# Layer 1's first modulation chunks and the context's keys and values, computed in the experts' stage instead of the tail

## The chip, the cores and the metric

One NeuronCore of a Trainium2 chip runs the whole program. The metric is device time in microseconds of one execution, as the median of several; times inside an execution are read from a profile of one execution, in microseconds from its first instruction.

## The reference, cut to what matters

Two blocks of a model follow each other, on 256 tokens of width 1024, all in fp32. The first block ends in a mixture of 16 experts; its result x is normalised and enters the second block, which has two layers and a second stream of 256 tokens, the context. The context does not depend on x. Layer 0 uses an MLA attention, layer 1 a neighbourhood attention (NA):

```python
for i in range(DEPTH_2):                      # 2 layers
    need_ctx = i < DEPTH_2 - 1                # only in layer 0
    mod   = (silu(c) @ ada_w[i] + ada_b[i])[:, None, :]
    mod_c = silu(c_ctx) @ ada_w[i] + ada_b[i]
    sh1, sc1, g1, sh2, sc2, g2 = split(mod, 6)       # and csh1, csc1, ... from mod_c
    h  = x * (1 + sc1) + sh1
    hc = ctx * (1 + csc1) + csh1
    y, yc = mixer(h, hc, ...)                 # layer 1: keys and values from h and from hc
    x = layer_norm(alpha * x + g1 * y)
    if need_ctx: ctx = layer_norm(alpha * ctx + cg1 * yc)
    x = layer_norm(alpha * x + g2 * mlp(x * (1 + sc2) + sh2))
    if need_ctx: ctx = layer_norm(alpha * ctx + cg2 * mlp(ctx * (1 + csc2) + csh2))

# NA mixer: qkv = t @ w_qkv + b_qkv for t = h and for t = hc; of hc only keys and values are used here
```

`ada_w[i]` is 1024 x 6144; the kernel cuts its columns into 12 chunks of 512. Chunks 0 to 3 are shift and scale of the attention (sh1, sc1), 4 and 5 its gate, 6 to 11 the same for the MLP. `w_qkv` is 1024 x 3072; the kernel cuts it into 4 pieces of 256 columns each for queries (part 0), keys (part 1) and values (part 2), 1024 KB a piece.

## The kernel before, in words

The program has three stages, and each engine works through its instructions in the order in which the program issues them.

- **Front** (`front`): first attention, router, layer 0's modulation.
- **Experts** (`experts`, line 1002): for each of 16 experts, gate and up weights in 8 pairs of 1408 KB tiles, then 11 tiles of 1024 KB of the down weights. All are loaded on SyncE's (SP's) queue through six buffers. Matmuls of 32 gathered rows (`egg`, `egu`, `ey`) use each tile once. Between them runs a generator, `ctx_stream` (line 1713): layer 0 for the context, that is MLA, output projection, norm, and the MLP. Its weights are loaded through `weight_loads` (line 304), four buffers `cwt` of 1024 KB, on GpSimd's queue. The generator is pulled in step with the experts: `context(units)` lets it take `CTX_STEPS` steps, spread evenly from expert 0's fifth pair to the start of the last expert. The matmuls of this stream are full-precision fp32. At its end the context is stored to DRAM as `ctx2`.
- **Tail** (`tail`, line 1906): what depends on x: layer 0's MLA and MLP, layer 1's NA and MLP. Here operands are split: a weight tile `cwt` is cast by ScalarE to a high part `wh` (L387), VectorE subtracts to get the low part `wl` (L388), activations have the same two parts, and `mm` (lines 176 to 178) issues three fp32r matmuls in place of one. Two or three places hold converted weights at a time (`slot`, `set_slots`, `weight`).

In the tail a second generator, `filler` (line 1767), is pulled between other work: four times in MLA (`MLA_PULLS`), once in its output projection (`PROJ_PULLS`), once in the hand-over to the MLP, then once for each step of the MLP. It computes layer 1's modulation (`ada`, line 426) with two buffers `adaw`: six chunks (`ADA_VECTOR`) on TensorE, one chunk a pull (8 matmuls `adap`, and 4 small ones `adac` that collect the chunk before), then six on VectorE, eight steps each. At its end it loads `ctx2` and makes the modulated context `hcT` (transposes `mtr`, ScalarE, GpSimd).

A hand-over between two parts of the tail is a `Between`: as output pieces of one part finish, VectorE adds the residual and takes the statistics; ScalarE normalises token half 0 (`xacc`, L1244); `finish` then transposes it (`mtx`), ScalarE and GpSimd make high and low parts (`hTx`), and the same follows for token half 1, with VectorE helping. `before()` and `between()` in `finish` are the places for other TensorE work. In the hand-over from the first MLP to NA they hold the context's value groups 0 and 1: `before` all of group 0, `between` all of group 1. After it come the values of x for these two weights, and then for each of the other two value weights and four key weights one group for the context and one for x (`na_proj`, tile `nqkv`), 48 matmuls of 256 columns each. Then come the queries and the attention itself.

Of the kernel before, what the change touches and what calls it, by code (L numbers as in the profile page):

```python
# [106 lines left out]
PROJ_PULLS = (0, 0, 1, 0, 0, 0, 0)  # L107
ADA_VECTOR = 6
# [5 lines left out]
CTX_STEPS = 109  # L114
# [42 lines left out]
def drain(gen):  # L157
    for _ in gen:
        pass


class Kernel:
# [141 lines left out]
    def weight_loads(self):  # L304
# [39 lines left out]
        mlp("c", 0, nc.gpsimd)  # L344
        lw.hold = len(lw.items)
# [79 lines left out]

    def ada(self, layer, pool, nbuf, loader, q, q2, vector=12):
# [4 lines left out]
        for ch in range(12):  # L431
# [12 lines left out]
        o, _ = COLS["adab"]  # L444
        bcol = self.cols[:, o + 48 * layer:o + 48 * layer + 48]

        def collect(ch, m, rhs):

            kind, half = divmod(ch, 2)
            nw = rhs.shape[1]  # L450
            p = self.bank(self.ada_tag, [128, 4, 2], "adac")
            for i in range(4):
                nc.tensor.matmul(p[:, i, :nw], m[:, i * 128:i * 128 + 128], rhs, start=True, stop=True)
            for i in range(nw):
                nc.vector.scalar_tensor_tensor(mod[:, ch * 4:ch * 4 + 4, i], p[:, :, i],
                                               1.0 if kind in (1, 4) else 0.0, bcol[:, ch * 4:ch * 4 + 4],
                                               op0=OP.add, op1=OP.add)
            if ch in (5, 11):
                gates.append(ch)
# [17 lines left out]
        for ch in range(vector):  # L477
# [1235 lines left out]
    def ctx_stream(self):  # L1713
# [48 lines left out]
        self.ctx2 = self.dram.tile([128, 2, D], F32, name="ctx2")  # L1762
        nc.gpsimd.dma_start(self.ctx2, x)
        yield


    def filler(self):
# [7 lines left out]
        c2 = None  # L1775
        for ch in ag:
            if ch == 4:
                self.modulation("c1a", 1, (0, 1), 1, "l2g0", "l2b0")
                self.modulation("x1a", 1, (0, 1), 0, "l2g0", "l2b0")
            if ch == ADA_VECTOR and c2 is None:  # L1780
                c2 = self.s8([128, 2, D], "c2")
                nc.scalar.dma_start(c2, self.ctx2)
            yield
        self.modulation("x1m", 1, (3, 4), 0, "l1g1", "l1b1")
        self.hcT = [self.fp.tile([128, 8, 256], F32R, name="hcT" + n, tag="adaw", bufs=2) for n in "hl"]
        t = self.cm["c1a"]
        for k in range(0, 8, 2):
            p = self.transpose_to(c2, k, 2, "c", "mtr")
            for j in (k, k + 1):
# [423 lines left out]
```

## Time and profile before

| | us |
|---|---|
| median of three runs | 2369.21 (2366.24 to 2371.48) |
| profiled execution | 2369.5 |
| its span, first to last instruction | 2367.4 |
| TensorE matmul busy | 2009.7 (85%) |
| VectorE busy | 801.4 (34%) |
| ScalarE busy | 552.3 (23%) |
| GpSimd busy | 253.6 (11%) |
| HBM read, over the span | 783.23 MB, 332 GB/s |

PE is TensorE's matmul side, PEld its weight load, DVE VectorE, ACT ScalarE, POOL GpSimd, SP SyncE. Busy times include what overlaps, so matmuls listed at 0.28 us may start every 0.12 us; starts tell more than durations. A full-precision fp32 matmul is listed as more than one record. The granted clock is the share of TensorE's full speed. L176 is line 176 of the kernel.

### The profile page before, as it was taken

To read this page: it belongs to the slowest core of one execution; us is meant where nothing else is said; L and a number is where in the kernel's file an instruction comes from. 1 tells how busy PE (TensorE), PEld (TensorE's weight loads), DVE (VectorE), ACT (ScalarE), POOL (GpSimd) and SP (SyncE) were. 2 spreads that over 40 slices of the span, in tenths; PEclk is the share of its full clock that TensorE was granted. 3 is DMA by queue.
4 is the path that set the end of the run, shared out by engine and by line. 5 is a ranking of instruction groups with operands and counts; after the bars stand their busy time and mean duration, and the time that the engine had idled before them with its cause. 6 is when DMAs were issued, how large, how long until landed. Compare 5 with 4: busy or idle time off the path is not lost.

```text
span 2367.4 us, 31973 instructions
## 1 busy us (share of the span) xinstructions
PE 2009.7 (85%) x13612; PEld 1244.8 (53%) x13612; DVE 801.4 (34%) x1471; ACT 552.3 (23%) x993; POOL 253.6 (11%) x274
## 2 busy tenths in 40 slices
PE   7998778787768877877878778678999999998998
PEld 6864324343214333332333333225888999987997
DVE  5643111121211111111111111214557765377555
ACT  5432011121000000000000000004444453276443
POOL 2021000000010000000000000003212113233001
PEclk9998888999968888988888889769999999999999
DMA  9879999999999999999999999998538864334652
GB/s 344 325 293 372 421 416 419 421 417 422 415 410 419 417 396 420 416 413 418 417 418 418 399 419 417 422 423 327 210 134 276 276 222 130 96 106 151 205 178 90
DMA packets 170006, 787.59 MB, mean 333 GB/s; under 512 B 13280, under 2 KB 73928, under 8 KB 113288
## 3 DMA queue, kind: packets, MB, share of 16 engines
q1 hardware_dynamic: 145432, 694.96, 74.1%
q0 software_dynamic: 24288, 89.54, 10.3%
q8 instruction: 107, 1.75, 0.3%
q10 hardware_dynamic: 144, 1.05, 0.1%
q14 instruction: 35, 0.29, 0.0%
HBM read 783.23 MB, written 2.27 MB: 332 GB/s over the span
## 4 chain that ended last, share of the span: by engine, by line
PE 46%; DMA 39%; DVE 3%; ACT 2%; issue 1%; DVEq 0%; ACTq 0%
DMA wg<-in_w_up 30%; DMA wd<-in_w_down 10%; PE egu L1045 4%; PE ey L1092 4%; PE acc L176 3%; PE acc L178 3%; PE acc L177 3%; PE ph L177 3%; PE ph L176 3%; PE ph L178 3%; PE py L174 2%; PE egg L1045 2%; PE ph L174 2%; PE nqkv L176 2%; PE nqkv L177 2%; PE nqkv L178 2%
## 5 line engine op out<-in xcount | busy, mean ns | idle before, releaser
L1045 PE MATMUL egu<-wg,xeT 128*32 128x352 f32 x2048 | 220.4, 557 | 112.3 <-DMA wg<-in_w_up 112.3
L388 DVE TENSOR_TENSOR wl<-cwt,wh 128x1024 fp32r<-128x1024 f32 (+1 forms) x202 | 249.1, 1276 | 57.0 <-ACT wh L387 56.8
L1092 PE MATMUL ey<-wd,hT 128*32 128x512 f32 x1408 | 197.6, 668 | 71.0 <-DMA wd<-in_w_down 70.5
L1045 PE MATMUL egg<-wg,xeT 128*32 128x352 f32 x2048 | 200.4, 514 | 62.4 <-DMA wg<-in_w_gate 62.3
L387 ACT CAST wh<-cwt 128x1024 fp32r<-128x1024 f32 (+2 forms) x218 | 214.7, 1035 | 91.3 <-issue 49.1
L1045 PEld LDWEIGHTS egu<-wg,xeT 128*32 128x32 f32 x2048 | 65.9, 123 | 246.6 <-DMA wg<-in_w_up 167.8
L1575 ACT ACTIVATE hu<-ph 128x512 f32<-128x512 f32 x48 | 28.7, 598 | 551.8 <-PE ph L174 442.1
L1045 PEld LDWEIGHTS egg<-wg,xeT 128*32 128x32 f32 x2048 | 57.5, 116 | 188.3 <-DMA wg<-in_w_gate 94.4
L176 PE MATMUL ph<-hTxh,wh 128*128 128x256 f32 x512 | 146.8, 287 | 1.6 <-ACT hTxh L1193 1.6
L177 PE MATMUL ph<-hTxl,wh 128*128 128x256 f32 x512 | 146.6, 286 | 0.6 <-DVE hTxl L1196 0.5
L178 PE MATMUL ph<-hTxh,wl 128*128 128x256 f32 x512 | 146.2, 286 | 0.0
L1092 PEld LDWEIGHTS ey<-wd,hT 128*32 128x32 f32 x1408 | 35.5, 115 | 195.2 <-DMA wd<-in_w_down 115.3
L1596 DVE TENSOR_TENSOR accc<-accc,py 128x512 f32<-128x512 f32 x60 | 41.3, 688 | 280.8 <-PE py L174 280.8
L174 PE MATMUL ph<-hcT,cwt 128*128 128x256 f32 x512 | 135.4, 423 | 0.0
L174 PE MATMUL py<-cwt,hs 128*128 128x512 f32 x256 | 132.5, 665 | 0.0
L174 PEld LDWEIGHTS ph<-hcT,cwt 128*128 128x128 f32 x512 | 106.5, 214 | 43.7 <-issue 27.6
L1578 DVE SCALAR_TENSOR_TENSOR hs<-ph,hu 128x512 f32<-128x512 f32 x16 | 11.1, 692 | 308.9 <-ACT hu L1575 308.9
L314 POOL DMA_DIRECT2D cwt<-in_w x32 | 25.8, 806 | 803.8 <-PE ph L174 334.4
L176 PEld LDWEIGHTS ph<-hTxh,wh 128*128 128x128 f32 x512 | 99.3, 194 | 2.8 <-ACT hTxh L1193 2.3
L177 PEld LDWEIGHTS ph<-hTxl,wh 128*128 128x128 f32 x512 | 99.2, 194 | 1.7 <-issue 0.7
L178 PEld LDWEIGHTS ph<-hTxh,wl 128*128 128x128 f32 x512 | 99.3, 194 | 0.0
L176 PE MATMUL acc<-wh,hsh 128*128 128x512 f32 (+1 forms) x256 | 97.8, 382 | 0.0
(562 smaller groups left out, 3491.9 us busy)
## 6 DMA issues: line engine op xcount, KB each, us to landing
wg<-in_w_gate SPq DMA_DIRECT2D x128, 1408.0 KB, 17.8
wg<-in_w_up SPq DMA_DIRECT2D x128, 1408.0 KB, 19.0
wd<-in_w_down SPq DMA_DIRECT2D x176, 1024.0 KB, 14.3
cwt<-in_w SPq DMA_DIRECT2D x64, 1024.0 KB, 5.3
cwt<-in_w POOLq DMA_DIRECT2D x32, 1024.0 KB, 13.7
adaw<-in_ada_w SPq DMA_DIRECT2D x24, 1024.0 KB, 9.2
adaw<-in_ada_w POOLq DMA_DIRECT2D x24, 1024.0 KB, 7.9
cwt<-in_w_in SPq DMA_DIRECT2D x12, 1024.0 KB, 10.5
```

Of the source, the lines that this page charges most:

```text
L174: t.matmul(out, L[0], R[0], start=start, stop=stop, **kw)
L176: t.matmul(out, L[0], R[0], start=start, stop=False, **kw)
L177: t.matmul(out, L[0], R[1], start=False, stop=False, **kw)
L178: t.matmul(out, L[1], R[0], start=False, stop=stop, **kw)
L314: q.dma_start(v, src)
L387: (high or nc.scalar.copy)(parts[0][:, s], t[:, s])
L388: (eng or self.low_eng).tensor_tensor(parts[1][:, s], t[:, s], parts[0][:, s].bitcast(F32), op=OP.subtract)
L1045: nc.tensor.matmul(ps[n][h][32 * j:32 * j + 32, :352], xeT[:, k, e * CAP:(e + 1) * CAP], w[:, c0:c0 + 352], start=k == 0, stop=k == 7, ski ...
L1092: nc.tensor.matmul(py[h][32 * s:32 * s + 32, :], hT[:, r, q], w[:, u, h * 512:h * 512 + 512], start=n < 2, stop=n >= 9, skip_group_check=True)
L1575: nc.scalar.activation(u, p, AF.Relu)
L1578: nc.vector.scalar_tensor_tensor(h, p, 0.0, u, op0=OP.max, op1=OP.mult)
L1596: nc.vector.tensor_add(s, s, p)
```

## The change

Chunks 0 to 3 of layer 1's modulation leave the filler and become steps of the context stream, after its MLP. They are computed on TensorE as before, and the helper that collects a chunk is now shared (`ada_collect`). The filler's `ada` starts at chunk 4; chunks 4 and 5 are still done on TensorE, the rest on VectorE. The pulls stay where they are.

The context stream goes on: it modulates the context (`hcT3`, one fp32 part instead of two) and multiplies it with the four key and the four value pieces of `w_qkv`, in full-precision fp32. Keys get their bias and are split into high and low parts (`kc`), values get theirs (`vc1`), and all go to DRAM. The store of `ctx2` goes. `weight_loads` gets 16 more items for it, on GpSimd's queue. `CTX_STEPS` grows from 109 to 132.

In the tail the context's eight groups go, with the modulated context and its load. Three loads bring `vn` and `kc` from DRAM. In the hand-over to NA, `before` holds nothing, and `between` holds the first half (token half 0) of x's value groups 0 and 1; the second halves follow after the hand-over. The conversion of the weights for x stays.

```diff
--- before.py
+++ after.py
@@ -105,13 +105,14 @@
 ADA_PULLS = (0, 1, 0, 2, 0, 0, 2, 0, 0, 2, 0, 0, 1, 0, 1, 1, 1, 1)
 MLA_PULLS = (3, 9, 13, 16)
 PROJ_PULLS = (0, 0, 1, 0, 0, 0, 0)
+ADA_FIRST = 4
 ADA_VECTOR = 6
 WOUT_AT = (14, 15)
 
 UNITS = 11, 4, 8 * 11 + 11 * 4
 CTX_FROM = 5 * 11
 CTX_LEFT = 8 * 11 + 11 * 4
-CTX_STEPS = 109
+CTX_STEPS = 132
 
 
 class Loader:
@@ -342,6 +343,13 @@
             add(("f", "wout", i), (2, 1024), self.kp(a["w_out"], i * 256, 2, 0, 1024), nc.sync)
         mla("c", nc.gpsimd)
         mlp("c", 0, nc.gpsimd)
+        for ch in range(ADA_FIRST):
+            for h in range(2):
+                add(("c", "ada", ch, h), (4, 512), self.kp(a["ada_w"][1], h * 512, 4, ch * 512, 512), nc.gpsimd)
+        for part in (1, 2):
+            for i in range(4):
+                add(("c", "qkv", part, i), (8, 256),
+                    self.kp(a["na_w_qkv"], 0, 8, part * 1024 + i * 256, 256), nc.gpsimd)
         lw.hold = len(lw.items)
         mla("x", nc.sync)
         mlp("x", 0, nc.sync)
@@ -423,12 +431,27 @@
             o, w = COLS[n]
             nc.scalar.activation(self.sc32[:, :, i], self.cols[:, o:o + w], AF.Silu)
 
+    def ada_collect(self, layer, ch, m, rhs):
+
+        nc = self.nc
+        mod = (self.mod0, self.mod1)[layer]
+        o, _ = COLS["adab"]
+        bcol = self.cols[:, o + 48 * layer:o + 48 * layer + 48]
+        nw = rhs.shape[1]
+        p = self.bank(self.ada_tag, [128, 4, 2], "adac")
+        for i in range(4):
+            nc.tensor.matmul(p[:, i, :nw], m[:, i * 128:i * 128 + 128], rhs, start=True, stop=True)
+        for i in range(nw):
+            nc.vector.scalar_tensor_tensor(mod[:, ch * 4:ch * 4 + 4, i], p[:, :, i],
+                                           1.0 if ch // 2 in (1, 4) else 0.0, bcol[:, ch * 4:ch * 4 + 4],
+                                           op0=OP.add, op1=OP.add)
+
     def ada(self, layer, pool, nbuf, loader, q, q2, vector=12):
 
         nc = self.nc
         W = 6144
         w = self.a["ada_w"][layer]
-        for ch in range(12):
+        for ch in range(ADA_FIRST, 12):
             for h in range(2):
                 src = bass.AP(tensor=w.tensor, offset=w.offset + h * 512 * W + ch * 512,
                               ap=[[W, 128], [128 * W, 4], [1, 512]])
@@ -441,20 +464,9 @@
         yield
         mod = (self.mod0, self.mod1)[layer]
         sel = self.tab("sel")
-        o, _ = COLS["adab"]
-        bcol = self.cols[:, o + 48 * layer:o + 48 * layer + 48]
 
         def collect(ch, m, rhs):
-
-            kind, half = divmod(ch, 2)
-            nw = rhs.shape[1]
-            p = self.bank(self.ada_tag, [128, 4, 2], "adac")
-            for i in range(4):
-                nc.tensor.matmul(p[:, i, :nw], m[:, i * 128:i * 128 + 128], rhs, start=True, stop=True)
-            for i in range(nw):
-                nc.vector.scalar_tensor_tensor(mod[:, ch * 4:ch * 4 + 4, i], p[:, :, i],
-                                               1.0 if kind in (1, 4) else 0.0, bcol[:, ch * 4:ch * 4 + 4],
-                                               op0=OP.add, op1=OP.add)
+            self.ada_collect(layer, ch, m, rhs)
             if ch in (5, 11):
                 gates.append(ch)
 
@@ -474,7 +486,7 @@
                                      ap=[[128, 8], [2048, nw], [1, 128]]), r[:8 * nw])
 
         last = None
-        for ch in range(vector):
+        for ch in range(ADA_FIRST, vector):
             p = self.bank(self.ada_tag, [128, 512], "adap")
             gate_rows()
             for h in range(2):
@@ -1759,9 +1771,58 @@
         g2 = [self.row(self.modrow[0], (2 + 1) * 1024 + hf * 512, 512, 2) for hf in range(2)]
         yield from self.resid_norm(x, [acc[:, tt].rearrange("p (a b) -> a p b", a=2) for tt in range(2)], 0, 1, 1,
                                    lambda hf: g2[hf])
-        self.ctx2 = self.dram.tile([128, 2, D], F32, name="ctx2")
-        nc.gpsimd.dma_start(self.ctx2, x)
-        yield
+
+        sw = self.sw
+        for ch in range(ADA_FIRST):
+            p = self.bank("c", [128, 512], "adap")
+            for h in range(2):
+                t = self.lw.take(("c", "ada", ch, h))
+                for g in range(4):
+                    nc.tensor.matmul(p[32 * g:32 * g + 32, :], self.sc32[:, 4 * h + g, :], t[:, g],
+                                     start=h == 0, stop=h == 1, skip_group_check=True)
+                self.lw.done(("c", "ada", ch, h))
+            m = sw.tile([128, 512], F32, name="adam", tag="qn", bufs=2)
+            self.copy(m, p)
+            yield
+            self.ada_collect(1, ch, m, self.tab("sel"))
+        self.modulation("c1a", 1, (0, 1), 1, "l2g0", "l2b0")
+        self.modulation("x1a", 1, (0, 1), 0, "l2g0", "l2b0")
+        hT = self.fm(8, False, None, "hcT3")
+        yield from self.modulate(hT, x, "c1a", "c")
+        self.kc = [self.dram.tile([128, 8, 256], F32R, name="kc" + n) for n in "hl"]
+        self.vc1 = self.dram.tile([128, 2, D], F32, name="vc1")
+        for part in (1, 2):
+            for i in range(4):
+                if part == 2 and i % 2 == 0:
+                    b = self.row(a["na_b_qkv"], 2048 + i * 256, 512, 2)
+                w, f = self.weight(("c", "qkv", part, i), False)
+                p = self.bank("c", [128, 2, 256], "nkv")
+                for j in range(2):
+                    js = slice(j * 128, j * 128 + 128)
+                    for k in range(8):
+                        if part == 1:
+                            self.mm(p[:, j], [w[0][:, k, js]], [hT[0][:, k]], k == 0, k == 7)
+                        else:
+                            self.mm(p[:, j], [hT[0][:, k, js]], [w[0][:, k]], k == 0, k == 7)
+                    if j == 0:
+                        yield
+                f()
+                if part == 1:
+                    hi = sw.tile([128, 2, 256], F32R, name="nkh", tag="qn", bufs=2)
+                    lo = sw.tile([128, 2, 256], F32R, name="nkl", tag="mptS", bufs=2)
+                    for j in range(2):
+                        bk = self.col("bqkv", 8 + 2 * i + j)
+                        nc.scalar.activation(hi[:, j], p[:, j], AF.Identity, bias=bk)
+                        nc.vector.scalar_tensor_tensor(lo[:, j], p[:, j], bk, hi[:, j].bitcast(F32),
+                                                       op0=OP.add, op1=OP.subtract)
+                    nc.gpsimd.dma_start(self.kc[0][:, 2 * i:2 * i + 2], hi)
+                    nc.gpsimd.dma_start(self.kc[1][:, 2 * i:2 * i + 2], lo)
+                else:
+                    vs = sw.tile([128, 2, 256], F32, name="nv", tag="qn", bufs=2)
+                    c0 = i % 2 * 256
+                    nc.vector.tensor_tensor(vs, p, b[:, None, c0:c0 + 256].to_broadcast([128, 2, 256]), op=OP.add)
+                    nc.gpsimd.dma_start(self.vc1[:, :, i * 256:i * 256 + 256], vs)
+                yield
 
 
     def filler(self):
@@ -1772,26 +1833,9 @@
         next(ag)
         lf.pump()
         yield
-        c2 = None
         for ch in ag:
-            if ch == 4:
-                self.modulation("c1a", 1, (0, 1), 1, "l2g0", "l2b0")
-                self.modulation("x1a", 1, (0, 1), 0, "l2g0", "l2b0")
-            if ch == ADA_VECTOR and c2 is None:
-                c2 = self.s8([128, 2, D], "c2")
-                nc.scalar.dma_start(c2, self.ctx2)
             yield
         self.modulation("x1m", 1, (3, 4), 0, "l1g1", "l1b1")
-        self.hcT = [self.fp.tile([128, 8, 256], F32R, name="hcT" + n, tag="adaw", bufs=2) for n in "hl"]
-        t = self.cm["c1a"]
-        for k in range(0, 8, 2):
-            p = self.transpose_to(c2, k, 2, "c", "mtr")
-            for j in (k, k + 1):
-                f = self.tw.tile([128, 256], F32, name="fullc", tag="full", bufs=3)
-                nc.scalar.activation(f, p[:, j - k], AF.Identity, bias=t[:, 1, j:j + 1], scale=t[:, 0, j:j + 1])
-                nc.scalar.copy(self.hcT[0][:, j], f)
-                nc.gpsimd.tensor_sub(self.hcT[1][:, j], f, self.hcT[0][:, j].bitcast(F32))
-            yield
 
     def na_attention(self, q, kvc, kvx):
         nc = self.nc
@@ -2080,23 +2124,27 @@
                     ql.append(self.tw.tile([128, 4, 256], F32R, name="ql" + n, tag="t4" + n, bufs=1))
                 return qh[:, t], ql[t // 4][:, t % 4]
 
-            def context(part, i):
-                w, f = self.weight(("x", "qkv", part, i), True)
-                return self.na_proj(w, None, part, i, self.hcT, (kct, self.vn)[part - 1], "c"), w, f
-
-            gc, w0, f0 = context(2, 0)
-            gc1, w1, f1 = context(2, 1)
-            hT = bt.finish(0, "ln2_b", lambda: drain(gc), lambda: drain(gc1))
+            nc.sync.dma_start(self.vn, self.vc1)
+            for t, d in zip(kc, self.kc):
+                nc.gpsimd.dma_start(t, d)
+            ww = [self.weight(("x", "qkv", 2, i), True) for i in range(2)]
+            gv = []
+
+            def values():
+
+                for i, (w, f) in enumerate(ww):
+                    gv.append(self.na_proj(w, f, 2, i, bt.hT, v, "d"))
+                    next(gv[i])
+            hT = bt.finish(0, "ln2_b", between=values)
         with ExitStack() as e1:
             self.sw = self.pool(e1, "naw")
             att = self.na_attention(qt, (kct, self.vn), (kxt, v))
-            drain(self.na_proj(w0, f0, 2, 0, hT, v, "d"))
-            drain(self.na_proj(w1, f1, 2, 1, hT, v, "d"))
+            for g in gv:
+                drain(g)
             next(att)
             for part, dst in ((2, v), (1, kxt)):
                 for i in range(2 if part == 2 else 0, 4):
-                    gc, w, f = context(part, i)
-                    drain(gc)
+                    w, f = self.weight(("x", "qkv", part, i), True)
                     drain(self.na_proj(w, f, part, i, hT, dst, "d"))
                     pull(bt.rest, 2)
             nat = self.pool(e1, "nat")
```

## Rows read from the trace of the kernel before

**Rows 1.** Busy time by stage; columns: stage, length, engines, granted clock, DMA share, GB/s.

```profile
205.00:1590.00 1385.00, 1087.78 (x7011) 450.56 (x7006) 217.73 (x420) 94.36 (x202) 47.29 (x55) 0.86 1.01 416
...
1800.00:1970.00 170.00, 170.00 (x1093) 154.39 (x1092) 119.74 (x145) 79.96 (x102) 25.64 (x29) 1.00 0.75 252
...
1970.00:2066.00 96.00, 93.86 (x787) 93.42 (x786) 40.81 (x62) 29.10 (x50) 30.80 (x35) 1.00 0.34 104
...
2066.00:2150.00 84.00, 78.44 (x805) 68.32 (x804) 63.09 (x149) 64.19 (x139) 24.49 (x28) 1.00 0.31 88
```

**Rows 2.** Waits: engine and line, what it waited for, us, times, longest.

```profile
PE egu L1045 <- DMA wg<-in_w_up: 112.3, 70, 3.5
...
PE ey L1092 <- DMA wd<-in_w_down: 70.5, 56, 3.0
```

**Rows 3.** DMA queues of 546 to 606: packets, MB, share of 16 engines.

```profile
q1 hardware_dynamic: 2941, 25.18, 100.6%
```

**Rows 4.** The same for 886 to 1328.

```profile
q1 hardware_dynamic: 18997, 165.14, 90.3%
q0 software_dynamic: 4887, 18.84, 10.7%
```

**Rows 5.** The same for the whole execution.

```profile
q0 software_dynamic: 24288, 89.54, 10.3%
```

**Rows 6.** Timeline of TensorE in the experts' stage: start, length, what, records.

```profile
1444.69 3.72 PE L174 MATMUL ph<-hcT,cwt 128*128 128x256 f32 x16
...
1595.55 1.38 PE L1092 MATMUL ey<-wd,hT 128*32 128x512 f32 x8
```

**Rows 7.** Timeline of TensorE from the MLP's last matmul to the third context group.

```profile
1969.66 0.28 PE L176 MATMUL nqkv<-wh,hcTh 128*128 128x256 f32 x1
...
1975.40 1.04 PE L1178 MATMUL mtx<-tabs,xacc 128*128 128x128 f32 x8
...
1981.97 0.60 PE L1178 MATMUL mtx<-tabs,xacc 128*128 128x128 f32 x4
...
1994.86 0.28 PE L176 MATMUL nqkv<-wh,hcTh 128*128 128x256 f32 x1
```

**Rows 8.** Timeline of ScalarE and VectorE among the key projections.

```profile
2031.46 0.47 ACT L1706 ACTIVATE kxh<-nqkv,cols 128x256 fp32r<-128x256 f32 x1 [4.20 <-PE nqkv L178]
...
2033.93 2.36 DVE L388 TENSOR_TENSOR wl<-cwt,wh 128x1024 fp32r<-128x1024 f32 x2 [0.45 <-ACT wh L387]
```

**Rows 9.** Timeline of ScalarE and GpSimd in the hand-over.

```profile
1973.00 1.24 ACT L1244 ACTIVATE xacc<-xacc,bmv 128x1024 f32<-128x1024 f32 x1 [0.43 <-DVE bmv L1243]
...
1981.05 0.74 POOL L1196 TENSOR_TENSOR hTxl<-full,hTxh 128x256 fp32r<-128x256 f32 x1 [0.41 <-ACT hTxh L1193]
...
1986.33 0.73 POOL L1196 TENSOR_TENSOR hTxl<-full,hTxh 128x256 fp32r<-128x256 f32 x1 [0.56 <-DVE hTxh L1193]
```

**Rows 10.** Busy time of 4 us after two other hand-overs.

```profile
1780.00:1784.00 4.00, 3.84 (x19) 3.87 (x20) 3.84 (x5) 3.19 (x4) 0.74 (x1) 0.57 0.98 380
...
2172.00:2176.00 4.00, 2.82 (x13) 2.18 (x14) 2.38 (x8) 3.04 (x8) 2.31 (x3) 0.63 0.76 255
```

**Rows 11.** Timeline of TensorE: modulation chunks, what follows one, context transposes.

```profile
1690.68 1.92 PE L483 MATMUL adap<-adaw,sc 128*32 128x512 f32 x16
...
1693.45 1.07 PE L1473 MATMUL mpt<-tabs,meb 128*128 128x128 f32 x8
...
1759.91 1.92 PE L483 MATMUL adap<-adaw,sc 128*32 128x512 f32 x16
...
1772.89 1.99 PE L483 MATMUL adap<-adaw,sc 128*32 128x512 f32 x16 [0.20 <-ACT full L1186]
...
1937.04 0.60 PE L246 MATMUL mtr<-tabs,c 128*128 128x128 f32 x4
```

**Rows 12.** DMA issues: times, KB each, median us from issue to landing.

```profile
cwt<-in_w POOLq DMA_DIRECT2D x32, 1024.0 KB, 13.7
...
cwt<-in_na_w_qkv SPq DMA_DIRECT2D x12, 1024.0 KB, 5.3
```

## The prediction

> **What bounds the kernel now.** I read the table of stages first [rows 1]. The kernel has three parts: a front that ends near 205 us, the experts' stage until about 1600, the tail. In the experts' stage (205 to 1590) the 16 DMA engines are busy all the time (share 1.01, 416 GB/s), TensorE only 1088 of 1385 us at a mean clock of 0.86. The waits say who is waited for: TensorE stood still for weight tiles, 112 and 71 us in the two longest [rows 2]. So this stage lasts as long as its bytes take, and TensorE has about 297 us to spare in it. The tail is the reverse: 170 of 170 us of TensorE in the second MLP part, 93.9 of 96 where queries, keys and values are projected, DMA at 0.31 to 0.75 [rows 1]. There every microsecond of TensorE work is one of the kernel, if the next work is ready.
>
> So the change moves work from where TensorE is the limit to where DMA is. It must be priced twice: bytes added to a stage that has no DMA time left, against matmul time taken out of the tail.
>
> **What it adds to the experts' stage.** Sixteen loads of 1024 KB (8 of modulation weights, 8 of key and value weights), 16.78 MB; two broadcast rows of 256 KB, 0.52 MB; twelve stores of 256 KB (key high and low parts, values), 3.15 MB; one store of 1024 KB, the old context, goes: 1.05 MB less. Net 19.4 MB, all on GpSimd's queue.
>
> The price of a byte there. In 546 to 606 only SP's queue runs: 25.18 MB in 60 us, 2.38 us/MB [rows 3]. In 886 to 1328 both run: 165.14 MB of SP's cost 165.14 x 2.383 = 393.5 us, so the 18.84 MB of GpSimd's queue took the other 48.5 us, 2.57 us/MB [rows 4]. They are of the same kind as the added ones (1 KB to 4 KB rows, 1024 KB each), so I take it: 19.4 x 2.57 = **49.9 us**. From below 2.38 us/MB, 46.2 us; from above the whole-kernel share of that queue, 10.3% of 2367.4 us for 89.54 MB [rows 5], 2.72 us/MB, 52.8 us. I exclude that they cost nothing, because no slice of that stage has DMA time free.
>
> The work that comes with them: a step of eight full-precision matmuls takes TensorE 3.72 us (16 records) [rows 6]; eight weights of two steps make 59 us, four modulation chunks of 2.77 us (below) 11. That is 70 of 297 us to spare, and it costs nothing as long as the loads stay the limit; without that cover it is 70 us. On VectorE and ScalarE it is a few copies per step, beside 218 and 94 busy us of 1385 [rows 1]. The stream still ends at the last expert's start, since the step count that paces it and its steps both grow by 23. A store of keys waits for ScalarE and VectorE, and the next weight load stands behind it on GpSimd's queue; four buffers run ahead, so I put that at nothing.
>
> **What it removes from the tail.** (a) Context keys and values. One group is 48 matmuls. Durations (0.28 us) overlap, so I read starts: 1969.66 to 1975.40 is one group, **5.74 us** [rows 7]. Eight go, 45.9 us. Six of them stand in the dense run of projections: 6 x 5.74 = 34.4 us come back in full, if the conversion of the next weight still fits under the 5.74 us of the one group that is left to each weight. From the free slot (2031.46) to the last VectorE piece (2033.93 + 2.36) it takes 4.8 us [rows 8], so it just does; if VectorE is held up by another 0.9 us, the rest is paid six times.
>
> (b) The other two cover the hand-over from MLP to attention, and here the cover goes. Before: from 1969.66 to 1994.86 TensorE does two context groups, transposes and two value groups, 25.2 us, without a long stop [rows 7]. After: nothing is there at 1969.66. The normalised half is ready at 1973.00 + 1.24 = 1974.2 [rows 9]. The transposes may start there and not at 1975.40; the chain of ScalarE and GpSimd pieces, whose last lasts until 1981.79 [rows 9], ends 1.1 us earlier, 1980.7. The first half of value group 0 trails it (ends about 1981), the first half of group 1 follows (2.9), then the other transposes (1.1), near 1984 to 1985. From the start of these transposes to the last low half it took 1981.97 to 1987.06, 5.1 us [rows 7, 9]; so the second half of group 0 ends about 1989.2 and that of group 1 about 1992.1. The stretch shrinks by 2.8 us instead of 11.5. And TensorE has stood almost idle for some 11 us: after the like hand-overs the granted clock fell to 0.57 and 0.63 over 4 us (part of it at 1.2 GHz) [rows 10]. Half the clock doubles the 2.9 us of a half group; I take 2.3 of it as lost. So **0.5 us** is gained here, bounds -3 (both halves slow) and +2.8.
>
> (c) Modulation. The first four of the six chunks on TensorE go. One takes 1690.68 to 1693.45, 2.77 us [rows 11], four 11.1. But the pulls stay where they were, and the later ones now pull VectorE steps. Gone from TensorE are those at 1690.68 (in a softmax chain, where VectorE's rotation of the queries would be late next; I count 1 of 2.77), at 1759.91 (between output pieces, in full), at 1772.89 (inside the hand-over before the MLP, where TensorE waits for the normalised rows anyway; 0.5), and one among dense projections (in full): 1 + 2.77 + 0.5 + 2.77 = **7 us**, bounds 4 and 11.
>
> (d) The context's transposes, four sets near 0.5 us in the dense MLP [rows 11]: **2 us**.
>
> New in the tail are three loads of 1024 KB (keys twice, values), at a DMA share of 0.34; they are needed at the first scores, more than 60 us later. SP's and GpSimd's queues wait with them for the MLP input's buffers at most, free before the hand-over: nothing. If that cover were gone, 5.3 us each, what one load takes to land in this stretch [rows 12].
>
> Sum: 34.4 + 0.5 + 7 + 2 = 43.9 us out (38 to 50), 49.9 in (46 to 53). The profiled execution took 2369.5 us (span 2367.4), the median of three is 2369.2, the same for this purpose. 2369.5 + 49.9 - 43.9 = **2375.5 us**. What three runs can tell from no change is 0.2%, 4.7 us: faster is below 2364.5, slower above 2374.
>
> **Rivals.**
> A, the forecast: bytes are paid in full, the hand-over opens. 2371 to 2383. Chance 0.60; 0.47 of it above 2374.
>
> B, it ends faster: all removed matmul time comes back, because the hand-over closes up by itself (the values start as soon as the rows are there). 45.9 + 11.1 + 2 = 59 us out: 2360.4. It decides from 54.6 us on. For it: 6 of 8 groups lie in dense work. Against it: the 4.6 us from 1969.66 to 1974.2 in which nothing is ready. 0.13.
>
> C, no change: bytes at SP's price, the hand-over at its better bound and modulation at 9: 2369.5 + 46.2 - 48.2 = 2367.5. 0.16.
>
> D: loads pay their time to land, not their share: 16 x 5.3 = 85 us [rows 12] and about 7 for the rest, 2418. Against it: in the experts' stage loads took 13.7 us to land [rows 12] with all engines busy, so they overlap. 0.03.
> The Trainium skill has a rule that points this way ("DMA: Bandwidth & Descriptors", section "Anatomy of one DMA"): a fixed cost of some 2 us and bytes over 436 GB/s for each transfer. By it a load is an estimated 4.4 us, sixteen are 70 and not 43, and the sum would be near 2403. By that rule 27 us more than forecast would show; the trace doesn't bear it out, its 2.57 us/MB [rows 4] are 2.7 us for such a load.
>
> E: two modulation loads per step, at 13.7 us each [rows 12], are more than a step lasts (1385 us by 132 steps, 10.5); chunks 2 and 3 hold TensorE some 13 us each, and the experts behind it don't catch up: 2375.5 + 26 = 2401. Against it: TensorE is free a fifth of the stage, and six tiles wait in buffers. 0.06.
>
> F: the loads hide, the experts' stage stays as long: 2369.5 - 43.9 = 2325.6. Against it: share 1.01. 0.02.
>
> **Numbers.** Predicted 2375.5. The range 2362 to 2386 takes in A, C and half of B. Faster 0.13 + 0.02 = 0.15; same 0.13 + 0.16 = 0.29; slower 0.47 + 0.03 + 0.06 = 0.56.
>
> **What would show it.** The last expert's first down-projection near 1645 and not 1595.55 [rows 6], with DMA still at 1.0; the tail from there to the end some 44 us shorter; a TensorE idle stretch of 4 to 5 us right after the MLP, low clock behind it; 5.7 us for each weight in the key and value projections. Wrong if the experts' stage grows by clearly less than 46 us (a cheaper byte) or more than 53, if projections wait for the weight conversion (then slower still), or if values close the gap.

## The result, and the profile after

The changed kernel takes 2392.71 us in the median (2389.18 to 2395.99, four runs) against 2368.82 for the kernel before on the same chip: ratio 1.0101, interval 1.0089 to 1.0114. It is 23.9 us slower; 6 were forecast, and the range ended at 2386. The profiled execution took 2395.99 us (span 2394.2), 3.3 us over the median; what is known of these 3.3 is told below.

The stages of the changed kernel, columns as in [rows 1]:

```profile
205.00:1645.00 1440.00, 1152.31 (x7327) 499.19 (x7325) 231.84 (x456) 93.34 (x206) 68.11 (x84) 0.86 1.00 411
...
1865.00:2028.00 163.00, 163.00 (x1031) 147.14 (x1030) 113.19 (x137) 71.63 (x84) 17.71 (x20) 1.00 0.76 258
2028.00:2092.00 64.00, 54.61 (x403) 52.95 (x403) 37.70 (x51) 25.13 (x42) 33.04 (x35) 0.89 0.50 154
```

Its longest waits for weights, as in [rows 2]:

```profile
PE egu L1057 <- DMA wg<-in_w_up: 114.1, 75, 3.5
...
PE ey L1104 <- DMA wd<-in_w_down: 51.8, 37, 3.5
```

GpSimd's queue over the whole execution, as in [rows 5]:

```profile
q0 software_dynamic: 28240, 102.65, 11.6%
```

13.1 MB more on that queue: 19.4 more in the stage, 2.1 of reloaded keys more and 8.4 of modulation weights less in the tail. So the bytes were counted rightly. But the stage (to 1645) moves 411 GB/s, not 416, although it is still the one that waits for weights.

To split the 26.8 us between the spans I use one mark: the last expert's first scatter matmul, where the tail begins. Before:

```profile
L1926 PE MATMUL esc<-sgye x8: 592/592/592, 1618.4 to 1621.4; 128*128 128x512 f32 x8
```

After:

```profile
L1970 PE MATMUL esc<-sgye x8: 592/592/592, 1683.3 to 1686.3; 128*128 128x512 f32 x8
```

The stage ends **64.9 us later** (49.9 forecast; the last expert's first down-projection starts at 1659.1 where 1645 was named); from the mark to the end of the span the tail went from 749.0 to 710.9 us, **38.1 us shorter** (43.9 forecast). The larger miss is in the experts' stage, so most experiments are about that.

**Where the stage loses time.** I cut it into windows of 4 us and added up what is missing in the DMA share wherever it is under 0.93: before 2.8 us in 3 windows, after 9.9 us in 11. One such place, TensorE of the changed kernel where an expert turns from its gate/up tiles (`egg`, `egu`) to its down tiles (`ey`):

```profile
1076.53 2.58 PE L1057 MATMUL egu<-wg,xeT 128*32 128x352 f32 x16 [0.84 <-DMA wg<-in_w_up]
1079.04 5.37 PE L175 MATMUL py<-cwt,hs 128*128 128x512 f32 x8
1087.16 1.24 PE L1083 MATMUL eht<-tabs,hh 128*128 128x128 f32 x8 [2.75 <-DVE hh L1075]
...
1089.45 1.94 PE L1104 MATMUL ey<-wd,hT 128*32 128x512 f32 x8
1091.32 4.37 PE L175 MATMUL ph<-hcT,cwt 128*128 128x256 f32 x16
```

VectorE there:

```profile
1082.72 0.69 DVE L1608 TENSOR_TENSOR accc<-accc,py 128x512 f32<-128x512 f32 x1 [17.03 <-PE py L175]
1084.44 0.69 DVE L1608 TENSOR_TENSOR accc<-accc,py 128x512 f32<-128x512 f32 x1 [1.03 <-PE py L175]
1085.05 2.05 DVE L1075 TENSOR_TENSOR hh<-hh,egu 128x352 f32<-128x352 f32 x4
```

ScalarE had its factor of `hh` ready:

```profile
1075.76 0.46 ACT L1073 ACTIVATE hh<-egg 128x352 f32<-128x352 f32 x1 [0.66 <-PE egg L1057]
```

Engines and DMA in the next windows:

```profile
1086.00:1090.00 4.00, 2.42 (x15) 1.70 (x19) 2.34 (x7) 0.79 (x3) 0.00 (x0) 0.91 1.01 414
1090.00:1094.00 4.00, 4.00 (x17) 2.31 (x10) 0.23 (x1) 0.26 (x1) 0.00 (x0) 0.67 0.68 231
1094.00:1098.00 4.00, 4.00 (x32) 1.95 (x34) 0.00 (x0) 0.00 (x0) 0.00 (x0) 1.00 0.57 195
```

SyncE's waits from 1075 to 1110:

```profile
SPq L999 <- PE ey L1104: 17.7, 4, 11.9
```

Read them as a chain. The last `egu` ends at 1079.1, and both factors of `hh` are there. A step of the context (`py`) takes TensorE at 1079.04. VectorE takes its instructions in the order of issue, and the step's two sums (`accc`) were issued before `hh`; they wait for `py`, so `hh` begins at 1085.05, six us late. The first down tile is used at 1089.45, and a second step holds TensorE until 1095.6. All six weight buffers are full meanwhile, SyncE waits 11.9 us for one, and the DMA share falls to 0.57. The Trainium skill ("PSUM — Partial Sum Buffer", section "Engine vs sequencer instructions") calls VectorE's queue strictly first in, first out; these rows agree.

### The profile page after: what moved, and what is told of

The parts are those of the page before. It is cut to its first block, busy times and chain, and to the rows that moved or that the text cites. A ratio compares the mean times of both kernels' runs of the same rounds, so it can differ in the third digit from the quotient of the medians.

```text
span 2394.2 us, 31753 instructions
## 1 busy us (share of the span) xinstructions
PE 2031.6 (85%) x13484; PEld 1251.1 (52%) x13484; DVE 810.9 (34%) x1479; ACT 540.1 (23%) x973; POOL 264.9 (11%) x289
## 3 DMA queue, kind: packets, MB, share of 16 engines
q0 software_dynamic: 28240, 102.65, 11.6%
## 5 line engine op out<-in xcount | busy, mean ns | idle before, releaser
L1057 PE MATMUL egg<-wg,xeT 128*32 128x352 f32 x2048 | 207.4, 529 | 56.1 <-DMA wg<-in_w_gate 56.1
L175 PE MATMUL ph<-hcT,cwt 128*128 128x256 f32 x512 | 122.6, 394 | 0.0
L175 PEld LDWEIGHTS ph<-hcT,cwt 128*128 128x128 f32 x512 | 97.4, 195 | 36.6 <-issue 24.2
L179 PE MATMUL acc<-wh,hsl 128*128 128x512 f32 (+1 forms) x256 | 97.1, 379 | 0.0
## 6 DMA issues: line engine op xcount, KB each, us to landing
cwt<-in_w_in SPq DMA_DIRECT2D x12, 1024.0 KB, 10.7
```

The costliest lines, as they stand in the source:

```text
L175: t.matmul(out, L[0], R[0], start=start, stop=stop, **kw)
L179: t.matmul(out, L[1], R[0], start=False, stop=stop, **kw)
L1057: nc.tensor.matmul(ps[n][h][32 * j:32 * j + 32, :352], xeT[:, k, e * CAP:(e + 1) * CAP], w[:, c0:c0 + 352], start=k == 0, stop=k == 7, ski ...
```

## The experiments

The theory, T1: the stage lost more than the price of its bytes because steps of the context stand at these turns. The rival, T2: the added bytes are dearer than 2.57 us per MB. All times are medians; "stage" is the mark above in the profiled run, so it is the figure of one run, while runs of one kernel lie 1 to 9 us apart.

| kernel | median us (range) | ratio to before (interval) | stage |
|---|---|---|---|
| e_loads_only | 2389.16 (2384.25 to 2392.62) | 1.0090 (1.0077 to 1.0104) | 1676.4 |
| e_work_only | 2350.04 (2349.98 to 2351.36) | 0.9922 (0.9909 to 0.9936) | 1639.1 |
| e_turn_clear | 2378.25 (2376.04 to 2383.04) | 1.0042 (1.0030 to 1.0055) | 1668.3 |
| e_loads_sync | 2391.07 (2385.51 to 2392.96) | 1.0090 (1.0075 to 1.0105) | 1682.0 |
| e_before_turn | 2366.18 (2364.59 to 2368.37) | 0.9991 (0.9982 to 0.9999) | 1614.5 |
| e_before_crowd | 2408.11 (2403.92 to 2409.00) | 1.0163 (1.0149 to 1.0177) | 1657.1 |
| e_fill | 2377.51 (2376.97 to 2380.67) | 1.0042 (1.0028 to 1.0055) | 1667.5 |
| e_ada_only | 2384.06 (2383.40 to 2385.13) | 1.0065 (1.0052 to 1.0078) | 1636.5 |
| e_no_store | 2372.58 (2369.00 to 2377.85) | 1.0017 (1.0008 to 1.0025) | 1659.6 |
| e_turn_sync | 2383.09 (2379.75 to 2385.44) | 1.0056 (1.0044 to 1.0069) | 1674.7 |
| e_before_sync | 2372.17 (2369.29 to 2374.85) | 1.0013 (1.0004 to 1.0022) | 1623.1 |
| e_hh_clear | 2382.04 (2381.51 to 2383.95) | 1.0058 (1.0046 to 1.0070) | 1671.2 |

**e_loads_only**, bytes without most of the work:

```diff
-                for g in range(4):
+                for g in range(4 - 3 * h):
...
-                    for k in range(8):
+                    for k in range(1):
```

> The changed kernel, with all its added loads and stores but only a fraction of the added matmuls in the experts' stage (5 of 8 per modulation chunk, one of them narrow, and 2 of 16 per key/value chunk), so the modulation and the keys and values are not the reference's. Theory T1 (the added TensorE work comes late at the turn from gate/up to down of an expert, the six weight buffers fill and the transfers stop): the stage keeps only the price of the bytes, 19.4 MB x 2.57 = 50 us, the last scatter of the experts starts near 1668 instead of 1683, and the time is near 2378. Theory T2 (the added bytes cost more than 2.57 us per MB, 65 us / 19.4 MB = 3.35): nothing changes, 2390 to 2395.

Measured 2389.16, next to T2's 2390 to 2395 and 11 us from T1's 2378. T1 as I had put it was wrong in one point: taking away most of the added matmuls gave 3.5 us back, not 15, and the intervals of the two kernels overlap. The added matmuls are not what stands at the turns. In the changed kernel the first of them runs here:

```profile
1343.45 2.79 PE L1781 MATMUL adap<-cwt,sc 128*32 128x512 f32 x16
```

All 11 windows counted above lie before 1102. What stands at those turns are the old steps of MLA and MLP, now paced at 132 steps to the stream instead of 109, in this kernel as in the changed one. Its own windows lose 4.9 us in 5, all before 1102, where its work is that of the changed kernel, so the 3.5 us are partly or wholly the spread of runs.

**e_work_only**, work without the loads:

```diff
-        for ch in range(ADA_FIRST):
-            for h in range(2):
-                add(("c", "ada", ch, h), ...)
-        ... (8 qkv items)
+        add(("c", "ada", 0, 0), (4, 512), self.kp(a["ada_w"][1], 0, 4, 0, 512), nc.gpsimd)
```

> The changed kernel with all its added matmuls and stores, but one 1 MB load in place of the 16 added ones; the other 15 chunks are computed from the same tile, so the modulation and the keys and values are not the reference's. 15.7 MB are gone, 3.7 MB net stay. T1 (TensorE late at the turn): 3.7 x 2.57 = 10 us for the bytes and 15 us for the lateness, stage +25 us against before, time near 2352. T2 (dear bytes): 3.7 x 3.35 = 12 us, stage +12 us, time near 2340.

Measured 2350.04, T1's number. The stage still grows by 20.7 us for 3.7 MB net; by T2 it would be 12. Its 4-us windows lose 8.5 us in 11, nearly as in the changed kernel, without the added loads.

**e_turn_clear**, the same work and bytes, other places for the steps:

```diff
+            e, u = divmod(units - 1, UNITS[2])
+            u = min(u + 1, 77) + max(u + 1 - 96, 0)
-            want = CTX_STEPS * (units - CTX_FROM) // (UNITS[2] * NE - CTX_LEFT - CTX_FROM)
+            want = CTX_STEPS * (113 * e + u - CTX_FROM) // (113 * (NE - 1) - CTX_FROM)
```

> The changed kernel with the same work, but no step of the context's stream is put between an expert's last gate/up tile and its third down tile; the steps are spread over the other tiles. T1: the transfers no longer stop at the turns; of the 4-us windows under a DMA share of 0.93 (11 in the changed kernel, 9.9 us lost) few stay, and the time falls by 7 to 15 us, to 2378 to 2386. T2: 2390 to 2395.

Measured 2378.25: 14.5 us came back by moving steps alone. No 4-us window is under 0.93 any more. TensorE at the turn of the same expert:

```profile
1065.82 1.53 PE L1059 MATMUL egu<-wg,xeT 128*32 128x352 f32 x12
1068.60 2.95 PE L1085 MATMUL eht<-tabs,hh 128*128 128x128 f32 x11 [1.25 <-DVE hh L1077]
1071.48 2.71 PE L1106 MATMUL ey<-wd,hT 128*32 128x512 f32 x16
```

The stage as a whole:

```profile
205.00:1630.00 1425.00, 1145.60 (x7329) 494.60 (x7327) 232.32 (x456) 95.16 (x207) 68.09 (x84) 0.88 1.01 416
```

From the last `egu` to the first `ey` it takes 4.1 us, not 10.3, and the rate is back at the 416 GB/s of [rows 1]. The last `egu` of this expert ends at 1067.4, in the changed kernel at 1079.1: 11.8 of the 15.0 us between the two marks are there before the first added matmul runs. T2 falls as the main cause.

**e_hh_clear**, half of that edit (77 and 88 in place of 77 and 96, so that only the step before `hh` goes):

```diff
+            u = min(u + 1, 77) + max(u + 1 - 88, 0)
+            want = CTX_STEPS * (121 * e + u - CTX_FROM) // (121 * (NE - 1) - CTX_FROM)
```

> The changed kernel with only half of e_turn_clear's edit: no step of the context's stream after an expert's last gate/up tile, but steps again from its first down tile on. H1 (the loss lies in the products hh: VectorE takes its instructions in order, so hh stands behind the step's sums, which wait for the step's matmuls on TensorE; meanwhile no buffer comes free): this half brings nearly all of e_turn_clear's 14 us, 2378 to 2382. H2 (the loss lies in the steps between the first down tiles, which hold TensorE while all six buffers are full): it brings little, 2386 to 2393.

Measured 2382.04, H1's end: 10.7 of the 14.5 us. So most of the harm goes when the step ahead of `hh` goes. But that step alone doesn't explain it. In the kernel before, too, it takes over 9 us from the last `egu` to the first `ey` at 5 of the 15 turns (6 in the changed kernel), and its windows lose only 2.8 us in all. By the two pacings a step is issued ahead of `hh` at ten turns in either kernel; in the changed one another follows within the first three down tiles at all ten, in the kernel before at four. So it seems to take both; the other half of the edit (steps kept ahead of `hh`, none between the first down tiles) was not run.

**e_before_turn and e_before_crowd**, the kernel before with its turns cleared (the edit of e_turn_clear) and crowded:

```diff
+            u += 2 * min(max(u - 77, 0), 19)
+            want = CTX_STEPS * (170 * e + u - CTX_FROM) // (170 * (NE - 1) - CTX_FROM)
```

> The kernel before with the pacing of e_turn_clear: no step of the context's stream between an expert's last gate/up tile and its third down tile. T1 (what stands at the turn stops the transfers; it cost the kernel before only 2.5 to 2.8 us, in 2 or 3 windows): 2 to 4 us less, 2364 to 2367, and no 4-us window of the stage under a DMA share of 0.93. Rival (the other pacing helps for another reason, by as much as in e_turn_clear): 14 us less, 2354.

> The kernel before with the same work and the same bytes, but the steps of the context's stream crowded at the turns: the last gate/up tile pair and the first three down tiles count three times as much in the pacing as they did, so that some 5 steps stand there and not 2. T1: without one byte more the transfers stop at most turns, 15 to 30 us are lost, 2383 to 2398. Rival (the changed kernel lost its 15 us to dearer bytes): no change, 2365 to 2371.

Cleared: 2366.18, 2.9 us less, as T1 had it; the fastest of the kernels that compute the reference, though within the 0.2%. Two windows under 0.93 are left (0.90 and 0.85), where none was expected. Crowded: 2408.11, 39 us more without one byte or matmul added, beyond T1's 30; 32.8 us of DMA time are missing. (The edit counts the last pair and the first two down tiles threefold; 39 steps stand there over the 15 turns, 2.6 a turn and not some 5, and 17 in the kernel before.) One crowded turn, VectorE:

```profile
599.88 0.70 DVE L1537 TENSOR_TENSOR pyc<-pyc,row 128x512 f32<-128x512 f32 x1 [17.48 <-PE pyc L174]
...
604.41 2.06 DVE L1066 TENSOR_TENSOR hh<-hh,egu 128x352 f32<-128x352 f32 x4 [0.76 <-ACT hh L1064]
```

And engines and DMA:

```profile
598.00:602.00 4.00, 1.84 (x5) 0.53 (x3) 2.05 (x3) 0.00 (x0) 0.00 (x0) 1.00 0.93 385
602.00:606.00 4.00, 0.00 (x0) 0.00 (x0) 2.74 (x8) 2.40 (x4) 0.00 (x0) 0.81 0.07 29
606.00:610.00 4.00, 3.42 (x15) 2.30 (x19) 1.78 (x5) 0.83 (x3) 0.00 (x0) 0.50 0.00 0
```

Here a whole norm of the context stands ahead of `hh`; TensorE and DMA stand still together for some 4 us. This turn and one like it, at 1542, hold 18.8 of the 32.8 us. So the run shows that steps at the turns stop the transfers, not how much they cost in the changed kernel.

**e_loads_sync, e_turn_sync, e_before_sync**, the loads on SyncE's queue (first the 16 added ones; then, with clear turns, all of the stream's, after and before):

```diff
-                    self.kp(a["na_w_qkv"], 0, 8, part * 1024 + i * 256, 256), nc.gpsimd)
+                    self.kp(a["na_w_qkv"], 0, 8, part * 1024 + i * 256, 256), nc.sync)
 (the eight modulation loads likewise; in the other two also:)
-        mla("c", nc.gpsimd)
-        mlp("c", 0, nc.gpsimd)
+        mla("c", nc.sync)
+        mlp("c", 0, nc.sync)
```

> The changed kernel with its 16 added loads issued by SyncE, on the queue of the experts' weights, instead of by GpSimd. T2, if the price is that of GpSimd's queue: 16.8 MB at SyncE's 2.38 us per MB instead of 3.35, 16 us less, near 2376. T1: the time stays at 2390 to 2395, or grows, since the loads now stand behind those that wait for an expert's buffer.

> e_turn_clear with all loads of the context's stream (the 16 added ones and the 30 MB or so that were there before) on SyncE's queue. If a byte on GpSimd's queue really costs 0.3 us per MB more (a fit over the stage's 20-us windows of the kernel before gives 2.38 us per MB for SyncE's and 2.62 to 2.77 for GpSimd's), 15 to 20 us go: 2358 to 2363. Rival (the fit only shows what moves beside these loads; e_loads_sync moved 16.8 MB and won 1.3 us in the stage): within 5 us of e_turn_clear, 2373 to 2381.

> e_before_turn with the loads of the context's stream on SyncE's queue. By the fit 46 MB x 0.3 = 14 us less than e_before_turn's 2366, 2352 to 2357, and then the fastest of all; by the rival 2361 to 2369.

The first changes nothing that can be told (2391.07). The other two are 4.8 and 6.0 us slower than their partners; only the second is clear of its partner's interval, and it is beyond both numbers expected for it. GpSimd's queue is not the dearer one here; the fit I had drawn the 0.3 us per MB from was wrong. Why SyncE's queue is slower with these loads was not settled.

**e_ada_only and e_no_store**, what the parts cost with clear turns: only the modulation moved; everything moved, but nothing stored. Against e_turn_clear the first puts back what the kernel before has for the context's keys and values, with `CTX_STEPS` at 113:

```diff
+        self.ctx2 = self.dram.tile([128, 2, D], F32, name="ctx2")
+        nc.gpsimd.dma_start(self.ctx2, x)
...
+        for ch in range(ADA_FIRST):
+            yield
...
-            hT = bt.finish(0, "ln2_b", between=values)
+            gc, w0, f0 = context(2, 0)
+            gc1, w1, f1 = context(2, 1)
+            hT = bt.finish(0, "ln2_b", lambda: drain(gc), lambda: drain(gc1))
...
```

The loop in the middle leaves the filler's first four pulls empty: chunks 4 and 5 stay late, where the kernel before has them. In the changed kernel they move up into MLA, so this run is not quite the change's first part in the tail.

The second:

```diff
-                    nc.gpsimd.dma_start(self.kc[0][:, 2 * i:2 * i + 2], hi)
-                    nc.gpsimd.dma_start(self.kc[1][:, 2 * i:2 * i + 2], lo)
...
-                    nc.gpsimd.dma_start(self.vc1[:, :, i * 256:i * 256 + 256], vs)
...
```

> Only the first part of the change: layer 1's modulation chunks 0 to 3 in the experts' stage; the context's keys and values in the tail as before (the turns kept clear as in e_turn_clear). By the terms: 8.4 MB x 2.57 = 21.6 us more in the stage, less the 3 us that the kernel before loses at its turns, and 7 us less in the tail: 2368 + 21.6 - 3 - 7 = 2380. Then keys and values alone, against e_turn_clear's 2378, are worth 2 us and the modulation is what makes the change slow. Rival E (two loads per step, 13 us each on TensorE, and the experts don't catch up): 2390 or more.

> e_turn_clear without the 3.1 MB of stores of keys and values in the stage; the tail reads 3.1 MB of a weight in their place, so its neighbourhood attention is not the reference's. With the turns clear, keys and values still cost the stage 31.8 us for 11.0 MB net (last scatter at 1668.3 against 1636.5 in e_ada_only). Theory P1 (every byte costs the same, 2.6 to 2.9 us per MB): 8 to 9 us less in the stage, 2369 to 2370. Theory P2 (a written byte is dearer: 8.4 MB of loads at 2.6 leave 10 us for 2.6 MB net of stores): 11 to 13 us less, 2365 to 2367.

The modulation alone makes the kernel 17.9 us slower than e_before_turn (2384.06 to 2366.18; 2380 was expected): the stage grows by 22.0 us (21.6 by the term), and up to the last MLP matmul the tail gives back only 4.2. Keys and values win 5.8 of it back (2384.06 to 2378.25), with the filler's shift in it. The stores cost the stage 8.7 us for 3.1 MB, 2.8 us per MB, P1's number; but that profiled run lies 3.2 us under its median, and the median fell by 5.7, less than either forecast. P2 falls by both.

**e_fill**, matmuls in the gap of the hand-over, on top of e_turn_clear:

```diff
-            hT = bt.finish(0, "ln2_b", between=values)
+            hT = bt.finish(0, "ln2_b", lambda: self.busy(10, "d"), values)
```

> e_turn_clear with 10 matmuls of 128x256 fp32, whose results nobody reads, in the gap that opened on TensorE between layer 0's MLP and the first transposes of the neighbourhood attention. If the half clock behind the gap (0.50 in the 8 us after it in the changed kernel) costs what the rows show, it goes and 3 to 5 us with it: 2373 to 2375. Rival (the clock behind the gap is hidden by the waits for ScalarE and for the weight conversion): within 1 us of e_turn_clear, 2377 to 2379.

Measured 2377.51, 0.7 us from e_turn_clear: the rival's number. TensorE:

```profile
2012.83 4.48 PE L197 MATMUL idle<-sc 128*128 128x256 f32 x20
2017.46 1.09 PE L1192 MATMUL mtx<-tabs,xacc 128*128 128x128 f32 x8 [0.16 <-ACT xacc L1258]
```

Busy times there, columns as in [rows 1]:

```profile
2016.60:2020.60 4.00, 2.18 (x14) 1.51 (x13) 3.69 (x9) 3.13 (x7) 0.72 (x1) 0.97 0.28 115
2020.60:2024.60 4.00, 4.00 (x22) 3.90 (x22) 1.20 (x4) 2.51 (x8) 2.19 (x3) 0.61 0.00 0
```

The gap was filled and the clock held through it, 1.00 and 0.97 (without the matmuls 1.00 and 0.64); then it fell all the same, to 0.61 under the first values.

## Why the prediction was wrong, point by point

The direction and the trade were right: bytes paid in full in one stage, matmul time saved in the other. **The step that failed** is the term for TensorE's work in the stage, put at nothing: "it costs nothing as long as the loads stay the limit", and the new step count, 132, was taken as harmless because the "stream still ends at the last expert's start". The first compares averages over the stage (297 us to spare), the second looks only at the stream's end. The spare time isn't free at every place: at a turn the stage hangs on one chain through TensorE, VectorE and TensorE, and only six buffers stand between that chain and the transfers. What the runs showed in its place is 11.1 us more in the stage (11.6 by the medians, 14.5 won by clear turns in the changed kernel less 2.9 before). They come from where the steps stand, and mostly from old steps that the new count puts elsewhere: taking out most of the added matmuls gave only 3.5 back. Of the 15.0 us that clear turns take off the stage of the changed kernel, the windows under 0.93 hold 9.9; where the rest is was not found.

| term | forecast | measured |
|---|---|---|
| bytes in the stage | +49.9 (46 to 53) | +53.8: 1668.3 - 1614.5, turns clear in both |
| TensorE's steps in the stage | 0 | +11.1: 1683.3 - 1668.3 = 15.0, less the 3.9 (1618.4 - 1614.5) that the turns of before cost already |
| (a), (b) projections and hand-over | -34.9 | last MLP matmul to last key matmul: -32.1 in the profiled run, -37.0 with turns clear |
| (c), (d) modulation and context's transposes in the tail | -9 (6 to 13) | mark to last MLP matmul: -5.1, 350.3 in e_before_turn to 345.2 in e_turn_clear; -6.6, 351.0 to 344.4, in the profiled runs of the two kernels |
| rest of the tail, with the three loads | 0 | +0.6 |

**The price of a byte**: 53.8 / 19.4 = 2.77 us per MB, 0.2 over the value taken and just over the upper bound of 2.72 [rows 5]. With clear turns no window is under 0.93, and the rate is 415 GB/s from 205 to the mark against 417 in e_before_turn, so the mechanism held. Why the added bytes cost more than the 2.4 us per MB of that average was not settled: it is not GpSimd's queue, by e_loads_sync; the size of packets (3.7 KB on average on GpSimd's queue in this stretch, 8.4 KB on SyncE's) was not tested. By the Trainium skill's fixed cost for each transfer ("DMA: Bandwidth & Descriptors", section "Anatomy of one DMA") the time would have been an estimated 27 us over the forecast sum. No run here shows a fixed cost of that size: with the turns clear 2378.25 was measured, 2.7 over it.

**The hand-over.** The gap is there as forecast (4 to 5 us):

```profile
2027.71 0.40 PE L179 MATMUL acc<-wh,hsl 128*128 128x512 f32 x1
2032.58 1.97 PE L1190 MATMUL mtx<-tabs,xacc 128*128 128x128 f32 x8 [4.47 <-ACT xacc L1256]
2035.80 0.58 PE L177 MATMUL nqkv<-wh,hTxh 128*128 128x256 f32 x1 [1.25 <-ACT full L1198]
```

The low clock behind it, in the changed kernel (0.50 is 1.2 GHz for the whole window, 1.00 is 2.4):

```profile
2032.00:2036.00 4.00, 2.17 (x9) 1.77 (x10) 3.73 (x9) 2.67 (x7) 0.72 (x1) 0.50 0.33 135
2036.00:2040.00 4.00, 4.00 (x19) 4.00 (x20) 1.09 (x2) 2.62 (x8) 2.19 (x3) 0.50 0.00 2
2040.00:2044.00 4.00, 4.00 (x30) 4.00 (x29) 0.00 (x0) 0.00 (x0) 0.00 (x0) 0.80 0.00 0
...
2048.00:2052.00 4.00, 4.00 (x21) 4.00 (x22) 0.70 (x2) 0.63 (x1) 3.85 (x7) 0.57 0.09 25
```

And in e_turn_clear, the same place:

```profile
2021.50:2025.50 4.00, 4.00 (x19) 4.00 (x20) 1.22 (x4) 2.72 (x8) 2.19 (x3) 0.51 0.00 0
2025.50:2029.50 4.00, 4.00 (x36) 4.00 (x35) 0.00 (x0) 0.00 (x0) 0.00 (x0) 1.00 0.00 0
```

From the last MLP matmul to the last key matmul it takes 64.0 us in the changed kernel's profiled run and in e_work_only, 60.2 to 60.6 in the seven others with all of the change, which shows in the rows as low clock twice instead of once. With six groups at their 34.4, (b) is a loss of 2.3 us in the profiled run and a gain of 2.6 with the turns clear, both inside its bounds. The 3.5 us between the two would be enough to put the profiled run above the median, but that the other runs lack them is not shown (e_work_only's profiled run has them and lies only 1.3 us above its others); what decides between the two was not found. **The weight conversion** fits under one group from 2060 on, as forecast: TensorE has no wait there, and the four key groups take 22.8 us from the first to the last start of their matmuls, 5.7 each. Right behind the hand-over it did not fit: at the third value weight TensorE waited for it, 2.6 us in the profiled run and 1.8 with the turns clear, which the forecast has not:

```profile
2056.39 0.39 PE L178 MATMUL nqkv<-wl,hTxh 128*128 128x256 f32 x1 [1.80 <-DVE wl L396]
2058.87 0.39 PE L178 MATMUL nqkv<-wl,hTxh 128*128 128x256 f32 x1 [0.80 <-DVE wl L396]
```

**Modulation in the tail** came out near its lower bound: 4.2 with the chunks left in place (e_ada_only), and 5.1 to 6.6 together with the transposes in the change itself.

**The rivals.** B and C ask for a cheaper byte or a closed hand-over: neither came. D and F are out by the rate. E has the nearest time, 2401, but not the cause: its own experiment gives +22.0 us in the stage, the price of the bytes. TensorE does wait for modulation loads in the changed kernel, 9.0 us in two waits, and the transfers go on meanwhile. The same work and bytes with clear turns gave 2378, inside the range; the turns took it out.

## What to carry to other kernels

An engine's spare time in a stage bound by transfers is cover only where the buffers can bridge its next lateness: look for the place where the stream's own chain is longest (here the turn between two weight kinds, 4 us of chain, six buffers) and keep fillers off it. A filler costs more than its matmuls: whatever it queues on another in-order engine ahead of the chain counts too. A new step count moves every step of the stream, the old ones too, so look where they come to stand. And price each part of a move by itself: here keys and values won 5.8 us once the turns were clear, and the modulation that they need lost 17.9.

## What the runs showed of the hardware that was not expected

Filling a 4.5 us gap with matmuls did not keep the clock: 1.00 and 0.97 in the gap's two windows, 0.61 in the next, after a further wait of 1.7 us for ScalarE. And one queue for all loads was slower than two: the stage lasted 8.6 us longer (1623.1 against 1614.5) with the same bytes, and the median was 6.0 us higher.
